# A shorter zero store and five loads split by partition parity in a DMA-bound SwiGLU

## Chip, cores, metric

The kernel runs on one core of one Trainium2 chip. The metric is device time in microseconds (us); lower is better.

## The reference

```python
# x: float32, 8192 x 8192
a, b = np.split(x, 2, axis=-1)
silu_b = b / (1 + np.exp(-b))
return a * silu_b            # 8192 x 4096
```

256 MiB in, 128 MiB out, two operations per element: the task is to move the data.

## The kernel before

x is taken as 32 tiles of 128 partitions x 64 KB (two rows of x side by side in each partition), with three buffers. SyncE issues the loads, ScalarE the stores; they are two DMA queues on the same 16 DMA engines (the page before: 68.6% and 31.2% of the engines' time). The product is written over the first half of the tile, so a tile's buffer is free for the next load when its store has landed (the loads' line waits for a store 29 times here, 868.6 us in all). A load or store counts as landed when its semaphore, the counter for which the other engines wait, has been raised for the sixteenth time. In the packet records each transfer's rows are followed by completion records, packets of 4 bytes: the trace before has 1072 of them, 67 transfers x 16, and as many raises, in the median 0.35 us after the record (the last store's last record starts at 932.68 us, its last raise is at 933.018). Landing times, and the times below of a store's or a first part's last records, are those of the raises.

```python
R = 2; BUFS = 3                     # M = 8192, half = 4096, P = 128
xv = x.tensor.reshape([N // R, R * M]).ap()
ov = out.tensor.reshape([N // R, R * half]).ap()

def load(i, rows=None):
    ...
    nc.sync.dma_start(
        out=tiles[i][:, lo * M : hi * M], in_=xv[i * P : (i + 1) * P, lo * M : hi * M]
    )

def store(i, c0=0, cw=R * half):
    (nc.scalar if i < last - 1 else nc.sync).dma_start(
        out=ov[i * P : (i + 1) * P, c0 : c0 + cw], in_=tiles[i][:, c0 : c0 + cw]
    )
...
nc.vector.memset(zt, 0.0)                       # zt is 128 x 128
nc.scalar.dma_start(out=ov[0:P, 0:128], in_=zt) # overwritten later by the store of tile 0

for i in range(BUFS):
    load(i)
for i in range(last):
    for k in range(R):
        swiglu(i, k)                            # Silu on ScalarE, product on VectorE
    ...
    store(i)
    nxt = i + BUFS
    if nxt < last:
        load(nxt)
    elif nxt == last:                           # the last tile in two halves
        ...
```

Of the kernel before, what the change touches and what calls it, by code (L numbers as in the profile page):

```python
# [1 line left out]

# [4 lines left out]

_SILU = mybir.ActivationFunctionType.Silu


@with_exitstack
def kernel(
    ctx: ExitStack,
    tc: tile.TileContext,
    x: bass.AP,
    out: bass.AP,
):




    nc = tc.nc
    N, M = x.shape
    half = M // 2
    P = nc.NUM_PARTITIONS
    R = 2
    BUFS = 3

    xv = x.tensor.reshape([N // R, R * M]).ap()  # L30
    ov = out.tensor.reshape([N // R, R * half]).ap()
    ntiles = N // (P * R)
    last = ntiles - 1

    pool = ctx.enter_context(tc.tile_pool(name="sbuf", bufs=BUFS))
    tiles = {}

    def load(i, rows=None):
        if i not in tiles:
            tiles[i] = pool.tile([P, R * M], x.dtype, name="xt")  # L40
        lo, hi = (0, R) if rows is None else rows
        nc.sync.dma_start(  # L42
            out=tiles[i][:, lo * M : hi * M], in_=xv[i * P : (i + 1) * P, lo * M : hi * M]
        )

    def swiglu(i, k, c0=0, cw=half):
        xt = tiles[i]
        b = xt[:, k * M + half + c0 : k * M + half + c0 + cw]
        nc.scalar.activation(out=b, in_=b, func=_SILU)  # L49
        nc.vector.tensor_mul(  # L50
            out=xt[:, k * half + c0 : k * half + c0 + cw],
            in0=xt[:, k * M + c0 : k * M + c0 + cw],
            in1=b,
# [5 lines that stand above are left out]
        )  # L59


    zt = ctx.enter_context(tc.tile_pool(name="zeros", bufs=1)).tile([P, 128], x.dtype, name="zt")
    ctx.enter_context(tc.manual_schedule())
    nc.vector.memset(zt, 0.0)  # L64
    nc.scalar.dma_start(out=ov[0:P, 0:128], in_=zt)

    for i in range(BUFS):
        load(i)
    for i in range(last):
        for k in range(R):  # L70
            swiglu(i, k)
        if i == last - 1:
            swiglu(last, 0)
# [4 lines that stand above are left out]
        elif nxt == last:  # L78
            load(last, (0, 1))
            load(last, (1, 2))  # L80

    store(last, 0, half)
    for c0 in range(0, half, half // 2):
        swiglu(last, 1, c0, half // 2)
    store(last, half, half)


# [1 line left out]
_INS = ['x']  # L89
_OUTS = [((8192, 4096), 'float32')]  # L90


# [23 lines left out]
```

## Time and profile before

| | before |
|---|---|
| median of the first 3 runs | 936.18 us (935.99 to 936.24) |
| span of the profiled run | 933.9 us |
| DMA busy, VectorE, ScalarE | 99.8%, 30%, 25% |
| rate in the steady stretch | 434 GB/s |

The prediction below shows the page's lines. These are three of six lines of the DMA issues (columns: out<-in, engine, operation, count, KB each, median us from issue to landing):

```profile
out_dram<-xt ACTq DMA_DIRECT2D x30, 4096.0 KB, 40.0
xt<-in_x_dram SPq DMA_DIRECT2D x31, 34.2
out_dram<-zt ACTq DMA_DIRECT2D x1, 64.0 KB, 24.1
```

A load lands 34 us after its issue and a store 40 us after its own. The chain of waits alternates load, compute, store, load on one of three buffers: 34 + 12.6 + 40 us makes some 87 us for three tiles, or 29 us a tile. Much of both times is waiting behind other packets: a load's own rows take 19.3 us of an engine, as the prediction works out (8 x 2.418), and a store's 9.7 us (8 x 1.213).

### The profile page before, as it was taken

The page shows a single profiled execution, that of the slowest core. Times are in us where ns is not written, and L with a number is a line of the kernel's source. Part 1 is how long each engine was busy: PE and PEld are TensorE (multiplying, and loading weights), DVE is VectorE, ACT ScalarE, POOL GpSimd, SP SyncE. Part 2 cuts the span into 40 slices and gives each one's busy share as a digit, 9 for nine tenths or more (in the row PEclk, how much of TensorE's full clock was granted, in tenths as well). Part 3 has the DMA queues.
Part 4 walks back from the last instruction along what each step waited for, and adds up shares of the span by engine and source line. Part 5 has one row for each costly group of instructions (what it writes and reads, how often), then busy time and mean ns, then how long its engine had stood idle before and what let it go on. Part 6 is the DMA issues. An engine that isn't in the chain of part 4 may idle for free.

```text
span 933.9 us, 370 instructions
## 1 busy us (share of the span) xinstructions
DVE 283.5 (30%) x66; ACT 229.4 (25%) x66; POOL 0.2 (0%) x4
## 2 busy tenths in 40 slices
DVE  0333312333113332133321333213332133331252
ACT  0323330233312333113331133311333203332041
POOL 0000000000000000000000000000000000000000
DMA  9999999999999999999999999999999999999998
GB/s 407 422 413 460 411 431 441 449 427 420 456 408 445 431 431 441 435 422 441 448 414 436 435 451 425 429 443 414 446 427 436 436 432 425 439 451 411 441 434 383
DMA packets 9650, 402.74 MB, mean 431 GB/s; under 512 B 1072, under 2 KB 1200, under 8 KB 1200
## 3 DMA queue, kind: packets, MB, share of 16 engines
q1 hardware_dynamic: 5184, 276.83, 68.6%
q10 hardware_dynamic: 4464, 125.90, 31.2%
q14 instruction: 2, 0.02, 0.0%
HBM read 268.44 MB, written 134.28 MB: 431 GB/s over the span
## 4 chain that ended last, share of the span: by engine, by line
DMA 84%; DVE 10%; ACT 4%; DVEq 0%; issue 0%; SPq 0%; ACTq 0%
DMA out_dram<-xt 43%; DMA xt<-in_x_dram 41%; DVE xt L50 10%; ACT xt L49 4%; DVEq L111 0%; SPq L42 0%; ACTq L49 0%; DVEq L50 0%
## 5 line engine op out<-in xcount | busy, mean ns | idle before, releaser
L50 DVE TENSOR_TENSOR xt<-xt 128x4096 f32<-128x4096 f32 (+1 forms) x65 | 283.3, 4360 | 635.8 <-ACT xt L49 632.6
L49 ACT ACTIVATE xt<-xt 128x4096 f32<-128x4096 f32 (+1 forms) x65 | 228.1, 3556 | 686.5 <-DMA xt<-in_x_dram 686.5
L49 ACT ACT_TABLE_LOAD x1 | 1.3, 1283 | 1.5 <-DVE zt L64 1.5
L64 DVE MEMSET zt<- 128x128 f32 x1 | 0.2, 165 | 0.8 <-PEq L100 0.8
L100 POOL MEMSET const-bfloat16-1.0<- 128x1 bf16 x1 | 0.1, 101 | 0.0
L100 POOL MEMSET const-uint8-127<- 128x1 uint8 x1 | 0.1, 101 | 0.0
L100 POOL MEMSET const-float32-0.0<- 128x1 f32 x1 | 0.1, 98 | 0.2 <-issue 0.2
L100 POOL MEMSET const-float32-1.0<- 128x1 f32 x1 | 0.1, 98 | 0.0
## 6 DMA issues: line engine op xcount, KB each, us to landing
out_dram<-xt ACTq DMA_DIRECT2D x30, 4096.0 KB, 40.0
xt<-in_x_dram SPq DMA_DIRECT2D x2, 4096.0 KB, 26.8
out_dram<-xt SPq DMA_DIRECT2D x1, 4096.0 KB, 23.6
out_dram<-xt SPq DMA_DIRECT2D x2, 2048.0 KB, 14.5
xt<-in_x_dram SPq DMA_DIRECT2D x31, 34.2
out_dram<-zt ACTq DMA_DIRECT2D x1, 64.0 KB, 24.1
```

Source lines behind the costliest of these rows:

```text
L49: nc.scalar.activation(out=b, in_=b, func=_SILU)
L50: nc.vector.tensor_mul(out=xt[:, k * half + c0 : k * half + c0 + cw], in0=xt[:, k * M + c0 : k * M + c0 + cw], in1=b,)
L64: nc.vector.memset(zt, 0.0)
L100: nc = _bacc.Bacc("TRN2", target_bir_lowering=False, num_devices=1)
```

## The change

Its intent: the zero store shrinks to one row per DMA engine (16 packets of 512 bytes, 128 before), and five more DMAs are issued, so that the kernel's last store takes the eighth of eight DMA semaphores, the one that is waited for last at the end (that wait is what the prediction calls the tail). The trace before shows the eight: three with 144 raises, five with 128, and SyncE's four waits at the end name them two by two. The five extra DMAs come from splitting the loads of tiles 3 to 7 into even and odd partitions.

```diff
-        nc.sync.dma_start(
-            out=tiles[i][:, lo * M : hi * M], in_=xv[i * P : (i + 1) * P, lo * M : hi * M]
-        )
+        step = 2 if BUFS <= i < BUFS + 5 else 1
+        src = xv[i * P : (i + 1) * P, lo * M : hi * M]
+        for p in range(step):
+            nc.sync.dma_start(out=tiles[i][p:P:step, lo * M : hi * M], in_=src[p:P:step, :])
...
-    zt = ctx.enter_context(tc.tile_pool(name="zeros", bufs=1)).tile([P, 128], x.dtype, name="zt")
+    zt = ctx.enter_context(tc.tile_pool(name="zeros", bufs=1)).tile([16, 128], x.dtype, name="zt")
...
-    nc.scalar.dma_start(out=ov[0:P, 0:128], in_=zt)
+    nc.scalar.dma_start(out=ov[0:16, 0:128], in_=zt)
```

## The prediction

Its sum, -0.19 + 0.045 - 0.13 = -0.28 us, gives 935.90 us. "The trace agrees for 128 rows" speaks of the completion records: 16 for each transfer. The first rival, also called the collision, is the estimate, that the measured 2.418 us of a packet in a split load could double. Of the second rival's 2 us for a gap, 1.0 us is measured; the rest was a guess at the landing.

> **What bounds the kernel now.** I read the page first (span, engines, DMA share), then the DMA part, then a table of stretches, then the waits of SyncE's queue and the last line's sequencer instructions. The page and its DMA part:
>
> ```profile
> span 933.9 us, 370 instructions
> DVE 283.5 (30%) x66; ACT 229.4 (25%) x66; POOL 0.2 (0%) x4
> DMA  9999999999999999999999999999999999999998
> DMA packets 9650, 402.74 MB, mean 431 GB/s; under 512 B 1072, under 2 KB 1200, under 8 KB 1200
> q1 hardware_dynamic: 5184, 276.83, 68.6%
> q10 hardware_dynamic: 4464, 125.90, 31.2%
> ```
>
> The two compute engines are idle 70% of the time. The two DMA queues together take 99.8% of what 16 engines have, in every slice but the last. Only something that makes the DMA engines carry less, carry it faster, or start sooner or stop later can move the time. The stretches show how flat it is (columns: stretch, its length, busy DVE, ACT, POOL, clock, DMA share, GB/s):
>
> ```profile
> 23.00:46.00 23.00, 8.85 (x2) 7.21 (x3) 0.00 (x0) 1.00 0.97 400
> 60.00:147.00 87.00, 26.55 (x6) 21.36 (x6) 0.00 (x0) 1.00 1.00 434
> 669.00:756.00 87.00, 26.55 (x6) 21.37 (x6) 0.00 (x0) 1.00 1.00 434
> 925.00:930.00 5.00, 0.00 (x0) 0.00 (x0) 0.00 (x0) 1.00 1.00 429
> 932.00:933.00 1.00, 0.00 (x0) 0.00 (x0) 0.00 (x0) 1.00 0.04 16
> ```
>
> Three tiles pass in 87 us: 3 x (8.39 MB in + 4.19 MB out) = 37.7 MB, 434 GB/s, and it stays so until the last store. In the packet records of the trace the first data packet starts at 1.74 us and the last ends at 932.69 us. Between them nothing is idle: the durations sum to 932.3 us per engine, a little more than the 931.0 us between those marks (packets of one engine overlap slightly at their ends). So only some 3 us, a head of 1.7 us and a tail of 1.2 us, is not transfer.
>
> By size, a load's row (64 KB) takes 2.418 us, a store's row (32 KB) 1.213 us, a 512-byte row of the zero store 0.027 us, and a 4-byte completion record 0.009 us (medians). The tail is where the title points:
>
> ```profile
> L111 SPq EVENT_SEMAPHORE  x6: 17/28/12459, 920.5 to 933.9; - x6
> L111 SPq DRAIN  x3: 7/7/7, 933.2 to 933.5; - x3
> SPq L111 <- DMA out_dram<-xt: 12.5, 1, 12.5
> ```
>
> After it has issued the last store, SyncE waits for all eight DMA semaphores, two per instruction, hence four wait instructions. In the instruction records they start at 920.51, 920.58, 933.08 and 933.14 us, the drain at 933.21. The second is the long one (12.459 us): it holds the last store's semaphore. The other two are already satisfied and cost only their own time.
>
> [...] The trace agrees for 128 rows: 67 DMAs x 16 = 1072 packets under 512 B. For 64 and 16 rows no run yet shows it. [...]
>
> **The change, part by part.**
>
> Zero store, 128 rows to 16: 112 packets of 512 bytes go, 7 per engine, 7 x 0.027 = 0.19 us of engine time, from the saturated resource. It now lands some 5 to 8 us after issue instead of 24.1 (an estimate: its one packet and its completion record take turns with two or three load packets of about 3.0 and 2.4 us, where eight turns were needed). Nobody waits for that: ScalarE's wait for it ended at 25.2 us, ten before the first store was ready at 35.40.
>
> Five loads (tiles 3 to 7) in two: 64 rows of 64 KB each, so the same 128 packets of the same size per tile. Five more DMAs bring 5 x 16 = 80 completion records, 5 per engine x 0.009 = 0.045 us. SyncE issues five more, 0.33 us each plus gaps. That is hidden:
>
> ```profile
> 69.83 58.32 SPq L42 DMA_DIRECT2D xt<-in_x_dram  x3
> 74.56 7.12 ACT L49 ACTIVATE xt<-xt 128x4096 f32<-128x4096 f32 x2 [21.75 <-DMA xt<-in_x_dram]
> ```
>
> The load of tile 3 is issued at 69.83, when the first store has landed, and the load before it lands only at about 74.5. So its ring has 4.7 us of work left, and the first half then gives 4 rows per engine before the second is needed. ScalarE must wait for two semaphores instead of one on five tiles, some 0.07 us each (28 ns plus a gap of 37 in SyncE's waits). The store that follows has 11.5 us of slack: store 1 is issued at 58.32, store 0 lands at 69.74 and the ring is never empty in between. Cost on the path: 0.
>
> The tail: now 33 loads + 33 stores + 1 zero store = 67 DMAs, dealt round eight semaphores. 67 = 8 x 8 + 3, so the last takes the third, and indeed three of the semaphores have 9 DMAs' completions in the trace and five have 8. After: 72 = 9 x 8, the last takes the eighth, which stands in the last of the four waits. Two satisfied waits move in front of the long one, where they cost nothing: from 933.08 to 933.21, 0.13 us.
>
> Sum: -0.19 + 0.045 - 0.13 = -0.28 us. 936.18 - 0.28 = 935.90 us. This is 0.03% and no larger than the 0.25 us spread of the three runs of before.
>
> **The rivals.**
>
> [...] For it: the landings of one load's 16 engines lie within 1.3 to 1.9 us in the trace, less than one packet, so engines are in step. [...] Cost if it is full: a load is 8 packets x 2.418 = 19.3 us per engine; doubled, five loads cost +97 us, 1033 us; if half is avoided, +48 us, 984 us. I give this about 11%; it is nearly the whole chance of "slower".
>
> Second, the second half of a load waits for the first to land (a dependence seen between the halves of one tile, or a semaphore reused too early). Then the load ring would run empty once per split load, for about 2 us each (1.0 us from issue at 0.73 to first packet at 1.74[...]). Five times is 10 us at worst, 946 us. But a store takes 40.0 us to land with one issued every 29 us, so the store ring has work in those gaps and takes the bandwidth; I would expect under 2 us to survive. Semaphore reuse speaks against: eight DMAs back, even with loads counted twice, is two to three tiles back and long landed. 5%.
>
> Third, the order of load and store packets shifts. A DMA's completion record takes a turn of the queue's alternation, so 5 more turns on the load queue give the stores a few packets earlier, and the last load and store may end in another phase: within one packet, 1 to 2.4 us at worst, either way, more likely a few tenths. This sets the width of the range.
>
> Fourth, a real gain of some per cent: the sum of packets stays at 930 us per engine, so no. 1%.
>
> **Range and chances.** The middle case gives 935.9 with a few tenths of phase and run noise. The low end is the sum plus 0.7 us of favourable phase, 935.2; nothing larger can be removed. The high end, 939.0, takes in an unfavourable phase and a mild form of the second rival; beyond it lies only the collision. Faster by over 2% (below 917): 1%. Slower by over 2% (above 955): 11%. Within 2%: 88%.
>
> **What would show it.** Right: 9618 packets, 1152 under 512 B and 1168 under 2 KB; the long SyncE wait of the last line is the fourth of four, with the drain 0.04 us after it; the stretch from 60 to 230 us still runs at 434 GB/s and the 64 KB packets there still take 2.418 us; the first half of a split load lands half a load ahead of the second. Wrong: 64 KB packets of 3 to 5 us in the stretch from 70 to 230 us (first rival); SyncE waiting for a load's landing ahead of a second half (second rival); a different end with the same packet sum (third); or a long wait still second of the four, where the semaphores are not dealt as I think.

## The result

| | before | after |
|---|---|---|
| median (6 runs each) | 936.09 us (935.84 to 936.24) | 939.33 us (938.89 to 939.68) |
| span of the profiled run | 933.9 us | 937.5 us |

The ratio is 1.0035 (95% interval 1.0022 to 1.0048): the changed kernel is 0.35% slower. The difference, 3.2 us, lies far outside the spread of either kernel, and just above the predicted range.

The page of the changed kernel, with its DMA part and issues:

```profile
span 937.5 us, 388 instructions
DVE 283.4 (30%) x66; ACT 229.4 (24%) x66; POOL 0.2 (0%) x4
DMA packets 9619, 402.69 MB, mean 430 GB/s; under 512 B 1152, under 2 KB 1168, under 8 KB 1168
q1 hardware_dynamic: 5264, 276.83, 68.6%
q10 hardware_dynamic: 4352, 125.84, 31.1%
...
out_dram<-xt ACTq DMA_DIRECT2D x30, 4096.0 KB, 34.3
...
xt<-in_x_dram SPq DMA_DIRECT2D x36, 39.8
out_dram<-zt ACTq DMA_DIRECT2D x1, 8.0 KB, 9.4
```

Packets are as predicted (9618 and one more of instruction fetch); 1152 completion records are 72 DMAs x 16, so transfers of 64 and of 16 rows have 16 records each too, which the prediction had to leave unshown. What nobody forecast stands in the issues: loads now land 39.8 us after issue and stores 34.3, the two have nearly changed places, and this is the median over all 36 loads, not only over the five that were split. The stretches of the changed kernel (columns as in the prediction):

```profile
60.00:147.00 87.00, 21.99 (x5) 21.37 (x6) 0.00 (x0) 1.00 0.99 419
147.00:234.00 87.00, 26.53 (x7) 21.37 (x6) 0.00 (x0) 1.00 1.00 433
669.00:756.00 87.00, 26.54 (x7) 21.37 (x6) 0.00 (x0) 1.00 1.00 434
```

From 60 to 147 us the DMA engines are busy 99% of the time and still move only 419 GB/s; from 234 us on the rate is again the old one. (A packet's bytes are counted whole, so a stretch of this length is good to about 1 MB, 12 GB/s.) The packet records, with each packet's bytes spread over its duration, say it exactly. Against the kernel before, in us of transfer at 434 GB/s, the changed kernel is behind by 0.4 at 60 us, 0.4 at 85, 1.4 at 100, 2.7 at 130, and 2.7 at every point from there to 920 us. I call this "the lag"; I give it at 900 us for every run below. Of the 2.7 us, 2.3 arise in two episodes, about 90 to 98 and 119 to 126 us. In them 46 of the 77 packets of 64 KB that start from 89 to 98 and from 119 to 126 us, at least one on each of the 16 engines in either, take 2.5 to 3.6 us instead of 2.418. The other 0.4 is there before the first split load is issued, at 69.86 us: it comes from the first store's meeting with the loads at 36 to 45 us, and over the runs below the lag at 60 us varies between -0.2 and 0.5. The rest of the 3.5 us between the two spans is unevenness of the engines: the 16 completion records of the last store come within 2.6 us of each other (before: 0.9), so the last engine is later than the average by more. Seen at the end, this too arises earlier. If the packets are joined to chains, one for each engine (as explained in the second group), the slowest engine of e8_one, the run with one split load, is 0.9 us behind the mean of all at 85 us and 2.0 us at 100: the episode does not slow all engines alike.

The timelines show the episodes from the side of ScalarE. Before, then after:

```profile
103.71 7.12 ACT L49 ACTIVATE xt<-xt 128x4096 f32<-128x4096 f32 x2 [22.03 <-DMA xt<-in_x_dram]
132.62 7.12 ACT L49 ACTIVATE xt<-xt 128x4096 f32<-128x4096 f32 x2 [21.79 <-DMA xt<-in_x_dram]
```

```profile
75.72 7.12 ACT L52 ACTIVATE xt<-xt 128x4096 f32<-128x4096 f32 x2 [21.88 <-DMA xt<-in_x_dram]
108.02 7.12 ACT L52 ACTIVATE xt<-xt 128x4096 f32<-128x4096 f32 x2 [25.18 <-DMA xt<-in_x_dram]
139.06 7.12 ACT L52 ACTIVATE xt<-xt 128x4096 f32<-128x4096 f32 x2 [23.91 <-DMA xt<-in_x_dram]
```

Tile 3, the first split one, is ready at 108.02 instead of 103.71, 32.3 us after tile 2 instead of 29.1; tile 4 another 31.0 us later instead of 28.9.

The tail did what it was built for. The last line of the changed kernel, and SyncE's waits for the same line:

```profile
L114 SPq EVENT_SEMAPHORE  x6: 17/28/28, 924.1 to 937.4; - x6
```

```profile
SPq L114 <- DMA out_dram<-xt: 12.4, 3, 4.8
```

The one wait of 12.459 us has become three, one for each of the last three stores, and the last store's is the last. From the last completion record to the drain it now takes 0.084 us (936.677 to 936.761) instead of 0.193 (933.018 to 933.211): 0.11 us gained.

### The profile page after: what moved, and what is told of

It reads as the page before. It is cut to its first block, busy times and chain, and to the rows that moved or that the text cites. A ratio compares the mean times of both kernels' runs of the same rounds, so it can differ in the third digit from the quotient of the medians. Undisturbed runs are those within 1.5% of the kernel's fastest.

```text
span 937.5 us, 388 instructions
## 1 busy us (share of the span) xinstructions
DVE 283.4 (30%) x66; ACT 229.4 (24%) x66; POOL 0.2 (0%) x4
## 2 busy tenths in 40 slices
DMA packets 9619, 402.69 MB, mean 430 GB/s; under 512 B 1152, under 2 KB 1168, under 8 KB 1168
## 4 chain that ended last, share of the span: by engine, by line
DMA 84%; DVE 10%; ACT 4%; issue 0%; DVEq 0%; SPq 0%; ACTq 0%
DMA xt<-in_x_dram 48%; DMA out_dram<-xt 36%; DVE xt L53 10%; ACT xt L52 4%; DVEq L114 0%; SPq L47 0%; ACTq L52 0%; DVEq L53 0%
## 6 DMA issues: line engine op xcount, KB each, us to landing
out_dram<-xt ACTq DMA_DIRECT2D x30, 4096.0 KB, 34.3
xt<-in_x_dram SPq DMA_DIRECT2D x36, 39.8
```

## Experiments

Sixteen runs, in four groups. "before" in each is the kernel before on the same chip in the same rounds. All outputs were correct.

| run | us | before | ratio (95%) | loads, stores land after | lag at 900 us |
|---|---|---|---|---|---|
| changed kernel | 939.33 | 936.09 | 1.0035 (1.0022 to 1.0048) | 39.8, 34.3 | 2.7 |
| e1_zero16 | 936.38 | 936.00 | 1.0002 (0.9987 to 1.0017) | 34.2, 40.0 | 0.1 |
| e2_split | 938.79 | 936.00 | 1.0028 (1.0013 to 1.0043) | 39.8, 34.3 | 1.5 |
| e3_cols | 939.11 | 936.00 | 1.0032 (1.0017 to 1.0047) | 39.8, 33.3 | 1.0 |
| e4_tiny | 936.24 | 936.00 | 1.0002 (0.9985 to 1.0019) | 33.7, 40.5 | -0.1 |
| e5_both | 936.60 | 936.04 | 1.0006 (0.9991 to 1.0021) | 34.5, 39.7 | 0.4 |
| e6_mid | 938.70 | 936.04 | 1.0029 (1.0014 to 1.0043) | 41.4, 32.8 at the end | 3.4 |
| e7_stores | 937.02 | 936.04 | 1.0012 (0.9997 to 1.0027) | 33.9, 40.3 | 0.9 |
| e8_one | 938.69 | 936.04 | 1.0027 (1.0010 to 1.0043) | 39.8, 34.5 | 1.4 |
| f1_tinyload | 936.41 | 936.07 | 1.0004 (0.9990 to 1.0019) | 40.0, 34.1 | 0.0 |
| f2_tinyboth | 936.34 | 936.07 | 1.0004 (0.9988 to 1.0021) | 34.2, 40.0 | 0.0 |
| f3_halves | 1025.68 | 936.07 | 1.0957 (1.0935 to 1.0979) | 39.8, 34.4 | |
| f4_oneboth | 936.35 | 936.07 | 1.0003 (0.9988 to 1.0018) | 34.3, 39.9 | 0.3 |
| g1_tiny_then_split | 935.97 | 936.16 | 1.0000 (0.9985 to 1.0015) | 40.9, 33.3 | 0.3 |
| g2_one_tinystore | 938.65 | 936.16 | 1.0026 (1.0009 to 1.0043) | 36.3, 37.9 | 1.9 |
| g3_one_late | 938.65 | 936.16 | 1.0028 (1.0013 to 1.0043) | 38.5, 35.7 | 2.1 |
| g4_four | 939.25 | 936.16 | 1.0035 (1.0020 to 1.0050) | 39.8, 34.4 | 2.6 |

The lag is of the profiled execution; the medians are over all. Single executions of the slower kernels differ by up to 1.8 us (e8_one: 937.78 to 939.41, g4_four: 938.51 to 940.33). What the lag leaves of a run's loss is in the spread of the engines: in e3_cols the last store's records lie 3.6 us apart, and it loses 2.9 us of span with a lag of only 1.0. The intervals are some 0.15% to either side, 1.4 us, so alone they leave room for a loss of 1 to 2 us in the runs that I call equal or free of cost. By that I mean a median within 0.6 us of the kernel before and a lag of at most 0.4 us.

### First group: which part of the change, and which kind of split

The first theory was that the split costs and the zero store does not; the rival, that the shorter zero store moves the moment at which the first store meets the loads, and all that follows.

**e1_zero16**, on the changed kernel:

```diff
-        step = 2 if BUFS <= i < BUFS + 5 else 1
+        step = 1
```

> The changed kernel without the split: only the zero store goes from 128 to 16 rows (67 DMAs, the last store on the third semaphore as before). Theory A (the split's extra completion records and doubled loads cost the 3.2 us): 935.9 us, no slow 64 KB packets outside the start and the first store. Rival B (the shorter zero store moves the phase in which the first store meets the loads, 1.6 us instead of 1.1 us of slow packets at 36 to 45 us, and all that follows): 938 to 939.5 us.

Measured 936.38 us, equal to before. The first store's meeting with the loads (slow packets from 36 to 45 us) costs 1.2 us per engine here and 1.1 before: it is in both kernels (1.6 in the changed kernel's trace, 0.9 in that of e2_split, so it varies from run to run). The rival falls. A gain of 0.15 us, as the sum had it for this part, is too small for these runs to show.

**e2_split**, the kernel before with the split alone (shown against the changed kernel):

```diff
-    ... .tile([16, 128], x.dtype, name="zt")
+    ... .tile([P, 128], x.dtype, name="zt")
-    nc.scalar.dma_start(out=ov[0:16, 0:128], in_=zt)
+    nc.scalar.dma_start(out=ov[0:P, 0:128], in_=zt)
```

> The kernel before with the split alone: the zero store keeps its 128 rows, five loads in two by parity, 72 DMAs. Theory A: 938.5 to 939.5 us, slow packets at about 85 to 126 us as in the changed kernel. Rival B: 936.1 us. If both parts matter: between, about 937.5.

938.79 us, with an episode at 88 to 98 us, a faint one at 120 us, and the landings of the changed kernel. The split is the cause. The stretch with the first episode, in e1_zero16 and then in e2_split:

```profile
60.00:147.00 87.00, 26.55 (x6) 21.37 (x6) 0.00 (x0) 1.00 1.00 434
```

```profile
60.00:147.00 87.00, 23.84 (x6) 21.37 (x6) 0.00 (x0) 1.00 1.00 426
```

**e3_cols**, split by rows of x and not by partition parity (with step = 1 in the load):

```diff
-            load(nxt)
+            if BUFS <= nxt < BUFS + 5:
+                load(nxt, (0, 1))
+                load(nxt, (1, 2))
+            else:
+                load(nxt)
```

> The changed kernel with the five loads split by rows of x (all 128 partitions, 32 KB each) and not by partition parity: the same 72 DMAs, the same number of completion records, but packets of 32 KB. If parity itself (rows two apart) costs: 936 us. If any split costs, by its completion records or because a load then takes smaller turns against the stores: 938 us or more.

939.11 us: parity is not what costs. But the way differs: its 32 KB packets take the queue's turn one for one against the store's 32 KB, the stores run ahead and their queue stands empty for several packets; slow packets are few and spread over 150 to 300 us, and most of the loss is the engines' spread. So equal times here do not show an equal mechanism.

**e4_tiny**, the eighth semaphore without a split (with step = 1 in the load):

```diff
-    nc.scalar.dma_start(out=ov[0:16, 0:128], in_=zt)
+    for j in range(6):
+        nc.scalar.dma_start(out=ov[0:16, j * 128 : (j + 1) * 128], in_=zt)
```

> No split; six zero stores of 16 rows instead of one, so that 72 DMAs are reached and the last store takes the eighth semaphore without touching the loads. Theory A: 935.8 us, and the semaphore's 0.13 us can be read in the last waits. Rival B: about 939 us as the zero store is still over early.

936.24 us. The last completion record is 0.109 us ahead of the drain (0.193 in e1_zero16), so the semaphore's gain of under 0.1 us is there, and it drowns in the spread of the runs. Five more DMAs by themselves, small ones at the start, cost nothing.

### Second group: turns

Next theory ("turns"): the engines alternate between the two queues. The trace before shows it: while both queues have work, an engine sends one packet of the one, then one of the other, and a packet is a single row (64 KB in 2.418 us or 32 KB in 1.213). It also shows that a completion record (0.009 us) takes a turn like a row. Below is the order of packets on one engine, put together by me from the packet records by joining each packet to the one whose end its start meets (not an output of the profile). L is a load row, S a store row, "." a load's completion record, "," a store's; a number is a duration in us where it is long.

```
before      S L , L S L S . S L S L S L S L S L S L , L S L S . S L
e8_one      L S L , L S . S L S L S L S L S . S L2.5 S L , L3.0 S L S . S L S L
f4_oneboth  L S L , L S . S L S L S L , L S . S L S L S L , L S . S L
f1_tinyload S L , L S L S . S L S L S L S L S L S L , L S L S . S z S . S L
```

Before, each tile has nine turns on each queue (8 rows, 1 record) and the order repeats exactly. A split load has ten: where its extra "." stands, the stores get a row ahead of their turn.

**e5_both**, the changed kernel with five stores split as well:

```diff
-        (nc.scalar if i < last - 1 else nc.sync).dma_start(
-            out=ov[i * P : (i + 1) * P, c0 : c0 + cw], in_=tiles[i][:, c0 : c0 + cw]
-        )
+        step = 2 if 1 <= i < 6 else 1
+        dst = ov[i * P : (i + 1) * P, c0 : c0 + cw]
+        for p in range(step):
+            (nc.scalar if i < last - 1 else nc.sync).dma_start(
+                out=dst[p:P:step, :], in_=tiles[i][p:P:step, c0 : c0 + cw]
+            )
```

> The changed kernel with five stores (tiles 1 to 5) split by parity as well, so that in the tiles concerned both queues have ten turns per engine (8 rows and 2 completion records) and not ten against nine. Turn theory (each extra completion record on the load queue hands the store queue one row ahead of its turn, 1.2 us per split tile, and the queues end up 6 us out of their old position): loads land in about 34 us and stores in about 40 us in the later tiles as before the change, time 936.0 to 936.8 us. Rival (each split DMA costs by itself, by its 64-row form or its issue): 939 us or more, up to 942.

936.60 us, landings back to 34.5 and 39.7. Ten transfers split cost less than five: a split DMA as such is not what costs.

**e6_mid**, the split in tiles 15 to 19:

```diff
-        step = 2 if BUFS <= i < BUFS + 5 else 1
+        step = 2 if 15 <= i < 20 else 1
```

> The changed kernel with the split moved from tiles 3 to 7 to tiles 15 to 19, in the middle of the steady stretch. Turn theory: the same shift there (stores land in 34 us instead of 40 after tile 19) and the same loss, 938.5 to 939.5 us. Rival (the split hurts only because it falls into the start, before the queues have settled after the first store): 936.0 us.

938.70 us, with no lag up to 415 us beyond that of e1_zero16, then two episodes at 436 to 446 and 466 to 476 us of 1.5 and 1.7 us. So the start is not needed for it.

**e7_stores**, loads whole, stores of tiles 1 to 5 split (the store edit of e5_both, with step = 1 in the load).

> Loads whole, the stores of tiles 1 to 5 split by parity (five more DMAs, on the other queue). Turn theory: the shift goes the other way, loads land in about 28 us and stores in about 46 us; the load ring has 4.7 us of reserve, so it comes near empty; the time should be 936 to 938 us, and in any case not the same picture as with split loads. Rival (any split DMA costs some 0.6 us by itself): 939 us with the landings unchanged.

937.02 us, and the ratio does not exclude 1. The forecast of the landings was wrong: a split store landed in up to 44 us for a tile, but the later ones land as before (33.9 and 40.3). A load cannot be issued before a store has landed; that may be why the shift in this direction undoes itself, which no run tests. Slow packets of up to 2.9 us at 107 to 112 us and a few up to 195 us raise the lag from 0.3 to 0.9 us. The profiled execution was the slowest of the four (938.00 us).

**e8_one**, only tile 3 split:

```diff
-        step = 2 if BUFS <= i < BUFS + 5 else 1
+        step = 2 if i == BUFS else 1
```

> The changed kernel with a single split load (tile 3) instead of five. If the loss goes with the number of splits: 936.6 us and a shift of 1.2 us (stores 39.2, loads 35.0). If the loss is all or nothing (the engines fall out of step once and stay so): 938 to 939 us. If the loss comes only once the store queue has lost all its reserve (several tiles): 936.0 us.

938.69 us, nearly the whole loss, and the whole shift of the landings (39.8 and 34.5), from one split load, that is, one extra completion record per engine. One episode at 89 to 98 us, 1.1 us of lag. So the cost does not add up from split to split, and the "1.2 us per split tile" of the turn theory is wrong. The page and the stretches:

```profile
out_dram<-xt ACTq DMA_DIRECT2D x30, 4096.0 KB, 34.5
...
xt<-in_x_dram SPq DMA_DIRECT2D x32, 39.8
```

```profile
60.00:147.00 87.00, 24.07 (x6) 21.36 (x6) 0.00 (x0) 1.00 0.99 422
147.00:234.00 87.00, 26.52 (x7) 21.37 (x6) 0.00 (x0) 1.00 1.00 434
```

So there is more than one steady order: loads at 34 and stores at 40 (call it A), and the reverse (B). Each keeps itself up, at the same 434 GB/s. B stands for a family: where nothing disturbs them, loads and stores stay at 38.5 and 35.6 in g3_one_late, at 41.4 and 32.8 in e6_mid, always some 74 us together.

### Third group: is it the shift that costs?

**f1_tinyload**, on the kernel before, nothing split:

```diff
+    lt = ctx.enter_context(tc.tile_pool(name="extra", bufs=1)).tile([16, 128], x.dtype, name="lt")
...
             load(nxt)
+            if nxt == BUFS:
+                nc.sync.dma_start(out=lt, in_=xv[0:16, 0:128])
```

> The kernel before, plus one load of 8 KB (16 rows of 512 bytes, one per engine, into a tile that nobody reads) on the load queue right behind the load of tile 3. No load is split. Per engine it adds one 0.027 us row and one completion record, so two turns, to the load queue. Turn theory: the later loads land in about 39.5 us and the stores in about 34.5 us as with one split load, time 938 to 939.5 us, though the bytes are a 50,000th. Rival (the cost is in the split load itself: its 64 rows, its longer issue, its two waits): 936.0 us and the landings unchanged (34 and 40).

```profile
out_dram<-xt ACTq DMA_DIRECT2D x30, 4096.0 KB, 34.1
...
xt<-in_x_dram SPq DMA_DIRECT2D x31, 40.0
...
lt<-in_x_dram SPq DMA_DIRECT2D x1, 8.0 KB, 36.2
```

Half of the turn theory holds, strikingly: 8 KB on the load queue move the later loads from 34 to 40 us (36.6 for the next one, 41.5 up to 415 us, 40.0 from 470). The other half falls: it costs nothing. 936.41 us, no episode, no lag, 438 GB/s from 60 to 147 us. Order B by itself is as fast as order A.

**f2_tinyboth**, with a tiny store besides (f1's edit and):

```diff
         store(i)
+        if i == 1:
+            nc.scalar.dma_start(out=ov[last * P : last * P + 16, 0:128], in_=zt[0:16, :])
```

> The same with one store of 8 KB as well, on the store queue behind the store of tile 1, so that both queues get two extra turns per engine in the same stretch. Turn theory: the two cancel, 936.0 to 936.7 us with landings of 34 and 40 us. Rival (any extra small DMA disturbs): as the tiny load alone or worse.

936.34 us, landings 34.2 and 40.0: two turns on each queue cancel in the order. In time there was nothing to cancel.

**f4_oneboth**, e8_one with the store of tile 1 split (the store edit of e5_both with `step = 2 if i == 1 else 1`).

> One split load (tile 3, 938.7 us by itself) with one split store (tile 1) beside it. Turn theory: one extra record on each queue cancels, 936.0 to 936.8 us, landings 34 and 40 us. Rival (the single split load costs by itself): 938.7 us or more.

936.35 us, order A kept, no slow packet after 60 us but two near 430 us, such as nearly every trace has between 360 and 470 us. One split load costs 2.7 us alone and nothing beside one split store.

**f3_halves**, contiguous halves and not parity:

```diff
-            nc.sync.dma_start(out=tiles[i][p:P:step, lo * M : hi * M], in_=src[p:P:step, :])
+            nc.sync.dma_start(out=tiles[i][p * P // step : (p + 1) * P // step, lo * M : hi * M],
+                              in_=src[p * P // step : (p + 1) * P // step, :])
```

> The changed kernel with the five loads split into partitions 0 to 63 and 64 to 127 and not by parity: the same 72 DMAs and completion records. If only the turns count: 939 us as the changed kernel. [...]loads in these tiles take up to twice as long: 64 KB packets of up to 4.8 us, and 955 to 1030 us.

The second case is the estimate from twice the measured 2.418 us.

```profile
60.00:147.00 87.00, 17.70 (x4) 14.25 (x4) 0.00 (x0) 1.00 1.01 326
147.00:234.00 87.00, 17.70 (x4) 14.24 (x4) 0.00 (x0) 1.00 0.99 285
234.00:415.00 181.00, 44.26 (x10) 35.62 (x10) 0.00 (x0) 1.00 0.97 363
500.00:900.00 400.00, 121.82 (x28) 99.73 (x28) 0.00 (x0) 1.00 1.00 434
```

1025.68 us, 90 us more, while the same number of DMAs and records by parity costs 3. The engines are busy 99% and move 285 GB/s; 64 KB packets take up to 6.1 us, more than the 4.8 expected. It is the slowing that the prediction's first rival feared, brought about by another split. No run shows the reason. By parity it is absent: tiles 5 to 7 of the changed kernel and all split tiles of e5_both have no slow packets to speak of.

### Fourth group: the split or the passage?

Open after twelve runs: does the episode belong to a split load, or to the queues' passage from order A to B by means of one?

**g1_tiny_then_split**, f1's tiny load behind tile 3 (with the zero store of 16 rows), then tiles 10 to 14 split:

```diff
-        step = 2 if BUFS <= i < BUFS + 5 else 1
+        step = 2 if 10 <= i < 15 else 1
```

> A tiny load of 8 KB behind the load of tile 3 (which shifts the landings to 40 and 34 us at no cost), then five loads split by parity, tiles 10 to 14. If the slow episode belongs to the passage from the old order of the queues to the new one: nothing is left to pass, 936.3 to 936.9 us, no slow packets after 45 us. If it belongs to a split load as such: 938.5 us or more, slow packets around the first halves' landings at about 290 to 420 us.

```profile
234.00:415.00 181.00, 54.31 (x13) 42.73 (x12) 0.00 (x0) 1.00 1.01 435
500.00:900.00 400.00, 121.69 (x28) 99.72 (x28) 0.00 (x0) 1.00 1.00 433
```

935.97 us: five loads split by parity, free. There are two slow packets after 60 us, as in the kernel before. The episode belongs to the passage by a split load, not to split loads.

**g2_one_tinystore**, e8_one with f2's tiny store:

> One split load (tile 3) with a tiny store of 8 KB on the store queue behind the store of tile 1 (two extra turns there against one on the load queue). If balance of the turns is what the split store restored: 936.0 to 936.9 us and landings near 34 and 40. If it was the second half store's being in the queue around the landing of the first half load that mattered: about 938.5 us as with the split load alone, with slow packets at 88 to 98 us.

938.65 us, with slow packets at 89 to 100 us; landings between the two orders (36.3 and 37.9). A tiny store at this place does not do what the split store did. It brings two turns against the split load's one, so the counts are not equal here, and the run does not decide whether f4_oneboth was spared by its equal turns or by its second half store.

**g3_one_late**, `step = 2 if i == 15 else 1`:

> One split load at tile 15 instead of tile 3. If one split anywhere gives one episode: 938 to 939 us, a loss of 1.0 to 1.7 us of bytes around 436 to 444 us and none elsewhere. If one split at tile 3 was special because the queues had just started: 936.1 us.

938.65 us, one episode at 437 to 447 us of 1.8 us, none elsewhere:

```profile
147.00:234.00 87.00, 26.55 (x6) 21.37 (x6) 0.00 (x0) 1.00 1.00 433
234.00:415.00 181.00, 53.10 (x12) 42.74 (x12) 0.00 (x0) 1.00 1.00 435
415.00:500.00 85.00, 26.55 (x6) 21.37 (x6) 0.00 (x0) 1.00 1.00 422
```

**g4_four**, `step = 4 if i == BUFS else 1`, every fourth partition:

> The load of tile 3 in four parts (every fourth partition, 32 rows each), three extra completion records in one tile. If the cost goes with the number of records: three episodes or one of three times the length, 941 us or more. If with the one passage of the queues: 938 to 939.5 us as with two parts.

939.25 us: three extra records cost about what one costs. The episode begins at the first quarter's end (83 us) and makes a lag of 2.1 us; its 64 KB packets take up to 4.3 us.

What stays open is why packets of all engines slow down in that passage. Known of it: each episode begins 1.5 to 4.5 us before a first part has landed on all engines (91.4 and 123.6 us in the changed kernel, 439.5 and 471.0 in e6_mid, 84.2 in g4_four), and it lasts some 8 to 10 us. A store is issued within 2 us of its beginning in the changed kernel and e6_mid (88.4, 120.7, 435.7, 468.0), but only 6 us after it in g4_four, so that is no condition. The full episode was seen with a split load while order A holds or is being left, and a weaker one with split stores (e7_stores). It is absent when the order is B already, when order B is reached by a tiny load at a tile's end, and when the store in the queue at that moment is split too. An empty store queue does not fit: in tiles 5 to 7 of the changed kernel the store queue runs dry for a packet without one slow packet to speak of. A clash between engines that lasts while a tile is split does not fit either, as it would go on in every split tile. One that ends once the engines have moved apart is not excluded; against it speaks that the split tiles of e5_both have no slow packets though the engines come no further apart in them (0.9 us between the first and the last at 60 us and at 130).

No run beats both kernels by more than the spread; g1_tiny_then_split (935.97, ratio 1.0000) equals the kernel before.

## Why the prediction was wrong

- **What bounds it** was right: no compute, no rate in the middle; 434 GB/s before and after.
- **Zero store**: no effect on the path that the runs can show (e1_zero16); the 0.19 us that the sum gave it is too small to be seen. Its landing was put at 5 to 8 us; it took 9.4.
- **Tail**: right. 0.13 us forecast, 0.11 seen in the records; e4_tiny shows it without the split. The sign named for it, one long wait in fourth place, came as three waits with the last store's in fourth place.
- **Split loads**: the issue is hidden, packets and records as counted. The failed step is "Cost on the path: 0" for this part, with 0.045 us as the only term. It should have been about 3 us (2.8 with the split alone, e2_split): 2.3 us of lag from two slow episodes in the changed kernel, and most of the rest in the engines' spread. The sum treated packet durations as constants; in the passage of the queues they are not. Why they are not stays open.
- **First rival** (packets of up to twice the length): with contiguous halves, which the change avoids, packets did take up to 6.1 us; not what happened here. Its sign, "64 KB packets of 3 to 5 us" from 70 to 230 us, did appear for two short episodes, so the sign alone would have pointed to the wrong rival. The 11% given to it was the wrong place for the doubt.
- **Second rival** (second half waits): absent. SyncE issues the second half 0.6 us after the first, 70.45 after 69.86 us.
- **Third rival** named the lever, an extra completion record taking a turn. It was sized at 1 to 2.4 us at the end, either way. In fact one tiny load, a row and a record, moves the landings by 6 us for the whole rest of the kernel, at no cost (f1_tinyload), and the cost came from what no rival had: slow packets in the passage, always to the worse.
- **Range**: 939.0 was 0.3 us too low. The class, within 2%, was right. Two slips that change nothing: the sum of -0.28 us is larger than the spread of 0.25 us, and store 1 has 11.4 us of slack (58.32 to 69.74), not 11.5.

## What to carry to other kernels

In this kernel, whose DMA engines are busy 99.8% of the time, two queues settled into an order of packets that repeats, and completion records are part of it: splitting one transfer on one queue tipped it into another order, and the passage cost more than the change was worth. In a kernel like it, judge a split there by its packet durations and landing times, not by its count of bytes and issues; and where a split is wanted, splitting the other queue's transfers in the same tiles kept the time here. Get a fraction of a microsecond at the end by means that leave the steady stretch alone, as the tiny stores did, though the 0.1 us gained there drowned in the spread of the runs. If a transfer must be split by partition, split by parity and not into contiguous halves: 0.35% against 9.6% here.
